# A two-layer decoder step: fewer plain head groups in the first attention stage, weight sums a stage later, the second chunk's norm in two passes through memory

## The chip, the cores and the metric

The kernel runs on one core of a Trainium2 chip. The time is device microseconds of one execution. A core has TensorE (matmuls, PE in the profile, its weight loads PEld), VectorE (DVE), ScalarE (ACT), GpSimd (POOL) and SyncE (SP). Each engine runs its own instructions in their order and waits on semaphores for the others. In this kernel SP starts the loads and the outputs, POOL starts nearly all stores to scratch memory.

## The reference

One step of a small decoder for 1024 prompt positions and 8 decode rows, model width 2048, in float32. Layer A: `z = x @ w_in`, half of z goes through causal pooling windows (2, 4, 8, 16) and a grouped projection, is gated by SiLU of the other half, and projected by `w_out`. Then `x = layer_norm(ALPHA * x + y)`. Its output gives one shared key and value (4 heads of 64). Layer B: queries and a gate from `z = h @ w_in_b`, sliding-window attention (128 keys) of 32 query heads with a learned sink, gate, projection and layer norm again:

```python
xp, sp = pool_layer(xp, prefix_p, pos_p, w_in_a[i], w_grp_a[i], scale_a[i], w_out_a[i], ln_g[i], ln_b[i])
k_p, v_p = shared_kv(xp, pos_p, w_kv)
xp = attn_layer(xp, pos_p, kb_p, vb_p, kpos_p, qpos_p, True, w_in_b[j], sinks_b[j], w_out_b[j], ln_g[i], ln_b[i])

def layer_norm(x, g, b):
    xf = x.astype(jnp.float32)
    mu = jnp.mean(xf, axis=-1, keepdims=True)
    var = jnp.mean(jnp.square(xf - mu), axis=-1, keepdims=True)
    return ((xf - mu) * lax.rsqrt(var + LN_EPS) * g.astype(jnp.float32) + b.astype(jnp.float32)).astype(x.dtype)
```

## The kernel before

**Chunks and phases.** Tokens lie along the free dimension, channels along the 128 partitions. The tokens are cut into chunk 0 (512) and chunk 1 (520: 512 and the 8 decode rows). `PHASES` (L50) lists ten phases in the order in which they run: input projection of layer A (`ai`), output projection of A (`ao`), input projection and attention of B (`bi`), output projection of B (`bo`). The third number of an `ai` or `bi` phase is the range of groups. A group of `bi` is four query heads and their gates: two pairs of weight rows, `wib` p (queries) and `wib` 8+p (gates), each pair four blocks of 128 x 1024.

**Exact matmuls in three.** Every weight block and every input tile is split into a rounded part (`hi`, a cast on ACT, L488 for weights) and the rest (`lo`, a subtraction on VectorE, L503 for weights). A block product is then three matmuls: hi by hi, hi by lo, lo by hi.

**Plain and seven products.** A plain unit (`unit`, L672 on) multiplies a block with all 512 tokens: 24 matmuls of 512 columns for each of a pair's four blocks (lines 686 to 688). A phase that is not in `PLAIN` uses a seven-product scheme for a 2 x 2 block product (`seven`, L582 on): seven weight blocks of 24 matmuls over half of the tokens, 256 or 260 columns (lines 658 to 660). Each has a post on ACT or VectorE that moves or combines the banks (L599 to L631). Three of the blocks are weights as they are, four are sums of blocks: `first_pair` (L332) makes the sums on VectorE from the loaded blocks (L346) and stores them in memory through POOL (L347). `plain_pair` (L300) makes and stores the same sums late (L293, L294) while the blocks are used plain. `next_pair` (L323) loads the sums in a later phase. The input of a seven-product phase needs four combinations too: `t_ops` (L820) makes them from a pair of tiles by four VectorE instructions (L826 to L829) and stores them through POOL (L830), `th` for the input of `bi`.

**Order.** `build_stream` lists all weight blocks in the order of use. At each block `begin` (L515) loads some blocks ahead (`load_to`), splits some ahead (`prep_to`: L503, `cast_to`: L488) and makes sums ahead. `end` (L527) runs events due at this block: the steps of the attention and, every `self.every` blocks, one step of the side generators, if enough slots are free. The side generator of this case is `ln_gen` (L912), the layer norm of a finished chunk. For chunk 1 it runs beside `bi` of chunk 0: mean, subtract (L962), square (L965), add (L968), variance, then for each of eight tile pairs multiply (L1000), affine on ACT (L991), store of the output through SP (L992) and `t_ops`. `in_order` ties PE, DVE and ACT to the source's order.

**Slots.** All working tiles come from 54 slots (`Mem`, L135) of 128 x 1040 floats. `full()` hands out the free slot that was let go longest ago; one that is being stored (`free(True)`) counts as let go ten turns later. The name of a tile in the order is `m`, the slot, the number of the allocation, and an id, so `m12_1836_16098` is slot 12. Who writes a slot anew waits for its last reader, a store included.

## Time and profile before

| | |
|---|---|
| median of 3 runs | 2332.18 us (2332.04 to 2333.17) |
| profiled execution | 2332.49 us, span 2330.7 us |
| TensorE busy, granted clock | 2293.2 us, 0.997 |
| VectorE busy | 1908.7 us |
| plain stage of `bi`, chunk 0 (4 groups) | 1080.6 to 1336.2 us |
| seven-product stage of `bi`, chunk 0 (4 groups) | 1336.2 to 1528 us |
| `bi`, chunk 1 | 1528 to 1961 us |

The busy time of TensorE is that of overlapping matmuls, so its pace is read from distances of starts, and its gaps from the idle time. The rows by stage give for each engine the busy time in a stretch. A group row gives the line, engine, tiles and shape, the count, the busy time and the mean of one, and behind the second bar the idle time before them and what ended it.

### The profile page before, as it was taken

The numbers are of one execution on the slowest core, as the hardware profiler recorded it, in microseconds if no ns is written. First come the engines' busy times: TensorE is split into PE (matmuls) and PEld (weight loads), VectorE is DVE, ScalarE is ACT, GpSimd is POOL, SyncE is SP. The second block draws the span as 40 slices with busy tenths as digits, with TensorE's granted clock in tenths as the row PEclk, the third lists the DMA queues.
The fourth block names the chain that finished last, engine by engine and source line by source line (L and its number), as shares of the span: only waits on it lengthen the run. The fifth ranks groups of instructions, "written<-read, shape, count | busy, mean of one in ns | idle before, by whom it ended". The sixth has DMA issues, their size and how long they took to land. (4 is left out here: it accounts for less than half of the span.)

```text
span 2330.7 us, 49775 instructions
## 1 busy us (share of the span) xinstructions
PE 2293.2 (98%) x19960; PEld 2199.7 (94%) x19960; DVE 1908.7 (82%) x2422; ACT 1350.4 (58%) x2492; POOL 205.7 (9%) x411
## 2 busy tenths in 40 slices
PE   8999999999999999999999999999999999999997
PEld 6899999999999999999788799999999999999997
DVE  8787998777878878988996888897676777889887
ACT  4444445544546546655465566785776678646556
POOL 0111110010000000000111111100000000000001
PEclk9999999999999999999999999999999999999999
DMA  8668789988899989999886666798777778799785
GB/s 293 221 228 312 267 293 356 330 302 297 278 325 320 340 280 325 323 385 345 274 333 240 241 220 236 240 321 288 246 245 221 221 229 307 243 361 379 250 303 198
DMA packets 250919, 665.04 MB, mean 285 GB/s; under 512 B 25760, under 2 KB 106432, under 8 KB 250688
## 3 DMA queue, kind: packets, MB, share of 16 engines
q1 hardware_dynamic: 205216, 496.79, 63.5%
q0 software_dynamic: 45472, 165.07, 18.4%
q8 instruction: 156, 2.56, 0.4%
q14 instruction: 75, 0.61, 0.1%
HBM read 466.66 MB, written 185.59 MB: 280 GB/s over the span
## 5 line engine op out<-in xcount | busy, mean ns | idle before, releaser
L658 PE MATMUL pD<-m,m 128*128 128x260 f32 (+1 forms) x4752 | 1346.2, 283 | 5.5 <-DVE m L619 3.9
L660 PE MATMUL pD<-m,m 128*128 128x260 f32 (+1 forms) x4752 | 1339.1, 282 | 3.3 <-DVE m L503 3.1
L659 PE MATMUL pD<-m,m 128*128 128x260 f32 (+1 forms) x4752 | 1339.3, 282 | 0.0
L658 PEld LDWEIGHTS pD<-m,m 128*128 128x128 f32 x4752 | 895.3, 188 | 10.9 <-issue 3.2
L660 PEld LDWEIGHTS pD<-m,m 128*128 128x128 f32 x4752 | 895.8, 189 | 4.0 <-DVE m L503 3.9
L659 PEld LDWEIGHTS pD<-m,m 128*128 128x128 f32 x4752 | 895.6, 188 | 0.5
L503 DVE TENSOR_TENSOR m<-m,m 128x1024 fp32r<-128x1024 f32 x674 | 814.6, 1220 | 72.7 <-ACT m L488 48.3
L488 ACT CAST m<-m 128x1024 fp32r<-128x1024 f32 x674 | 701.5, 1048 | 253.1 <-DVE m L346 77.7
L686 PE MATMUL pD<-m,m 128*128 128x512 f32 x448 | 179.7, 401 | 8.0 <-ACT m L769 8.0
L687 PE MATMUL pD<-m,m 128*128 128x512 f32 x448 | 177.6, 396 | 0.7 <-DVE m L778 0.7
L688 PE MATMUL pD<-m,m 128*128 128x512 f32 x448 | 177.2, 396 | 0.0
L778 DVE TENSOR_TENSOR m<-m,m 128x1024 fp32r<-128x1024 f32 (+1 forms) x120 | 147.1, 1229 | 9.5 <-ACT m L769 7.9
L631 ACT COPY m<-pD 128x260 f32<-128x260 f32 (+1 forms) x83 | 31.0, 374 | 189.8 <-PE pD L660 189.7
L769 ACT CAST m<-m 128x1024 fp32r<-128x1024 f32 (+1 forms) x120 | 125.8, 1051 | 10.3 <-DVE m L503 4.1
L346 DVE TENSOR_TENSOR m<-m,m 128x1024 f32<-128x1024 f32 x88 | 107.6, 1223 | 6.9 <-DMA m<-in_wia 4.2
L686 PEld LDWEIGHTS pD<-m,m 128*128 128x128 f32 x448 | 85.0, 190 | 27.9 <-ACT m L769 8.0
L687 PEld LDWEIGHTS pD<-m,m 128*128 128x128 f32 x448 | 85.0, 190 | 20.6 <-DVE m L778 1.9
L688 PEld LDWEIGHTS pD<-m,m 128*128 128x128 f32 x448 | 84.8, 189 | 19.8
L619 DVE TENSOR_TENSOR m<-pD,m 128x260 f32<-128x260 f32 (+1 forms) x86 | 36.5, 425 | 80.9 <-PE pD L660 80.8
L1798 ACT ACTIVATE m<-m,sm 128x128 f32<-128x128 f32 x256 | 99.2, 390 | 0.0
L1820 ACT ACTIVATE m<-m,sm 128x128 f32<-128x128 f32 (+1 forms) x320 | 93.9, 372 | 8.9 <-DVE sm L1806 5.5
L1088 PE MATMUL pD<-m,m 128*128 128x260 f32 (+1 forms) x528 | 91.2, 323 | 0.0
(249 smaller groups left out, 2157.2 us busy)
## 6 DMA issues: line engine op xcount, KB each, us to landing
m<-in_wia SPq DMA_DIRECT2D x124, 512.0 KB
m<-in_wib SPq DMA_DIRECT2D x120, 512.0 KB
swia<-m POOLq DMA_DIRECT2D x64, 512.0 KB, 5.0
m<-swia SPq DMA_DIRECT2D x64, 512.0 KB
m<-swoa SPq DMA_DIRECT2D x64, 512.0 KB
swib<-m POOLq DMA_DIRECT2D x64, 512.0 KB, 5.8
m<-swib SPq DMA_DIRECT2D x64, 512.0 KB
m<-swob SPq DMA_DIRECT2D x56, 512.0 KB
```

What stands on the lines that cost most here:

```text
L346: self.nc.vector.tensor_add(s[out].a[:, :1024], s[x].a[:, :1024], s[y].a[:, :1024])
L488: self.nc.scalar.copy(hi.r[:, :1024], self.stream[self.cast].src().a[:, :1024])
L503: self.nc.vector.tensor_sub(lo.r[:, :1024], s.src().a[:, :1024], hi.a[:, :1024])
L658: nc.tensor.matmul(ps[:, :TH], wh[:, s], h, start=new and k == 0, stop=False, skip_group_check=on)
L659: nc.tensor.matmul(ps[:, :TH], wh[:, s], l, start=False, stop=False, skip_group_check=on)
L660: nc.tensor.matmul(ps[:, :TH], wl[:, s], h, start=False, stop=k == 7, skip_group_check=on)
L686: nc.tensor.matmul(ps[:], wh[:, s], h, start=par == 0 and k == 0, stop=False)
L687: nc.tensor.matmul(ps[:], wh[:, s], l, start=False, stop=False)
L688: nc.tensor.matmul(ps[:], wl[:, s], h, start=False, stop=par == 1 and k == 7)
L769: self.nc.scalar.copy(h.r[:, :n], s.a[:, :n])
L778: self.nc.vector.tensor_sub(l.r[:, :n], s.a[:, :n], h.a[:, :n])
L1798: nc.scalar.activation(x["s3"][:, i, :], x["s3"][:, i, :], AF.Exp, bias=nm[:, i : i + 1], scale=0.125, accum_out=rs[:, i : i + 1],)
```

## The change

The first attention stage (`bi`, chunk 0) does groups 0 and 1 plain and groups 2 to 7 in seven products; before it was four and four. The plain groups no longer make their weights' sums. The stage of chunk 1 makes those of groups 0 and 1 itself, from the blocks, without storing them (`first_pair` with `keep=False`).

The norm of chunk 1 goes through memory: after the mean is subtracted and the square taken, tile pairs 0 to 6 are stored and let go. A second pass begins at count 56 after the phase's start (`self.i`, in which a plain block counts twice and a product of the seven once), that is 8 products into the seven-product stage. It loads the pairs again and for each pair does multiply, affine and `t_ops`, a step every 2.4 products.

`begin` now looks at free slots: it loads five blocks ahead and goes on to seven only while more than two slots are free, and splits one block less ahead with one slot free or none.

```diff
-    ("ai", 0, (0, 1)), ("ai", 0, (1, 4)), ("ai", 1, (0, 4)), ("ao", 0, None), ("ao", 1, None), ("bi", 0, (0, 4)),
-    ("bi", 0, (4, 8)), ("bi", 1, (0, 8)), ("bo", 0, None), ("bo", 1, None),
+    ("ai", 0, (0, 1)), ("ai", 0, (1, 4)), ("ai", 1, (0, 4)), ("ao", 0, None), ("ao", 1, None), ("bi", 0, (0, 2)),
+    ("bi", 0, (2, 8)), ("bi", 1, (0, 8)), ("bo", 0, None), ("bo", 1, None),
...
-    def first_pair(self, name, q):
+    def first_pair(self, name, q, keep=True):
...
-                self.nc.gpsimd.dma_start(ws[:, i, :], s[out].a[:, :1024])
+                if keep:
+                    self.nc.gpsimd.dma_start(ws[:, i, :], s[out].a[:, :1024])
...
-                if seven:
-                    for p in range(*part):
-                        w += pr("wib", p) + pr("wib", 8 + p)
-                else:
-                    for p in range(*part):
-                        q, g = pr("wib", p), pr("wib", 8 + p)
+                for p in range(*part):
+                    if not seven:
+                        q, g = ([self.lone(a) for a in self.quads("wib", n)] for n in (p, 8 + p))
                         w += q[:2] + g[:2] + q[2:] + g[2:]
+                        continue
+                    for n in (p, 8 + p):
+                        if c and p < PLAIN[1][2][1]:
+                            f = self.first_pair("wib", n, False)
+                            w += [f[i] for i in ORDER7]
+                        else:
+                            w += pr("wib", n)
...
         a, b, d = self.ahead if self.strassen else (5, 4, 3)
-        if getattr(self, "ph", "") == "bi1" and len(self.mem.whole()) < 3:
-            a, b, d = min(a, 6), min(b, 3), min(d, 2)
-        self.load_to(self.e + a)
-        self.prep_to(self.e + d)
-        self.cast_to(self.e + b)
-        self.make_to(self.e + b + (1 if self.strassen else 0))
+        free = lambda: len(self.mem.whole())
+        self.load_to(self.e + min(a, 5))
+        while self.loaded < min(self.e + a, len(self.stream)) and free() > 2:
+            self.load_to(self.loaded + 1)
+        self.prep_to(self.e + (d if free() > 1 else d - 1))
+        self.cast_to(self.e + (b if free() > 1 else b - 1))
+        self.make_to(self.e + (b if free() > 0 else b - 1) + (1 if self.strassen else 0))
...
                     nc.scalar.activation(flat(sqs[p - 1]), flat(pre[p - 1]), AF.Square)
+                    if p < 8:
+                        nc.gpsimd.dma_start(away(p - 1), self.pair_view(pre[p - 1], T))
+                        pre.pop(p - 1).free(True)
...
+        if c:
+            while self.i < self.mark:
+                yield
+            load(6)
...
+        if c:
+            turns = (6, 7, 0, 1, 2, 3, 4, 5)
+            for n, p in enumerate(turns):
+                if n < 7:
+                    load(turns[n + 1])
+                t = self.pair_view(pre[p], T)
+                nc.vector.tensor_mul(t, t, b2(rr))
+                yield
+                affine(p)
+                yield
+                self.t_ops(t[:, 0], t[:, 1], td, p, T // 2)
+                pre[p].free(True)
+                yield
...
             elif (kind, c) == ("bi", 0) and not self.strassen:
+                self.mark = self.i + 56
...
+            elif (kind, c) == ("bi", 0):
+                self.every, self.room = 2.4, 2
```

How VectorE's order changes is seen at two places. Lines 503, 826 to 829 and 1000 of before are lines 508, 832 to 835 and 1015 after the change. The first place is the second pass of the norm. Before, it stands in the plain stage, between plain blocks; `m51` holds the factor of the norm:

```order
L1000 TENSOR_TENSOR m24_1555_13007<-m24_1555_13007,m51_1536_12865 128x1040
L503 TENSOR_TENSOR m10_1627_13710<-m12_1617_13596,m16_1623_13665 128x1024
L826 TENSOR_TENSOR m44_1630_13736<-m29_1549_12967 128x260
L827 TENSOR_TENSOR m44_1630_13736<-m29_1549_12967 128x260
L828 TENSOR_TENSOR m44_1630_13736<-m29_1549_12967,m44_1630_13736 128x260
L829 TENSOR_TENSOR m44_1630_13736<-m29_1549_12967,m44_1630_13736 128x260
L1000 TENSOR_TENSOR m0_1562_13056<-m0_1562_13056,m51_1536_12865 128x1040
L503 TENSOR_TENSOR m41_1632_13764<-m3_1621_13661,m43_1628_13712 128x1024
```

Here the sums for `th` lie in slot 44, and the next split goes into slot 41. The second place is the fourth product of group 5, in the seven-product stage. Before:

```order
L1791 TENSOR_TENSOR sm_283_15815<-sm_282_15814,prm_75 128x8
L503 TENSOR_TENSOR m21_1810_15824<-m3_1787_15502,m35_1807_15786 128x1024
L503 TENSOR_TENSOR m39_1813_15862<-m22_1799_15655,m32_1811_15826 128x1024
L346 TENSOR_TENSOR m22_1799_15655<-m22_1799_15655,m3_1787_15502 128x1024
L1926 SCALAR_TENSOR_TENSOR m23_1798_15653<-m36_1808_15820,m23_1798_15653 128x1024
```

and after the change (L1818 is L1791 of before, L1953 is L1926):

```order
L1818 TENSOR_TENSOR sm_285_16057<-sm_284_16056,prm_75 128x8
L508 TENSOR_TENSOR m20_1834_16064<-m1_1812_15769,m36_1832_16028 128x1024
L832 TENSOR_TENSOR m12_1836_16098<-m29_1791_15501 128x260
L833 TENSOR_TENSOR m12_1836_16098<-m29_1791_15501 128x260
L834 TENSOR_TENSOR m12_1836_16098<-m29_1791_15501,m12_1836_16098 128x260
L835 TENSOR_TENSOR m12_1836_16098<-m29_1791_15501,m12_1836_16098 128x260
L508 TENSOR_TENSOR m12_1839_16110<-m32_1827_15985,m10_1835_16066 128x1024
L346 TENSOR_TENSOR m32_1827_15985<-m32_1827_15985,m1_1812_15769 128x1024
```

The four sums for `th` have moved in ahead of the split of this product, and the split writes slot 12, the one that they filled.

13 lines of the change are left out of this document (7 added, 6 removed).

## The prediction

> **What bounds the kernel now.** I read the page's busy shares first, then the table of stages, then what TensorE waits for in the two stages that the change touches.
>
> ```profile
> span 2330.7 us, 49775 instructions
> ...
> PE 2293.2 (98%) x19960; PEld 2199.7 (94%) x19960; DVE 1908.7 (82%) x2422; ACT 1350.4 (58%) x2492; POOL 205.7 (9%) x411
> ```
>
> TensorE (PE) is idle for 2330.7 - 2293.2 = 37.5 us of the span, so the whole kernel runs at TensorE's pace. The next table has one row for the plain attention stage of chunk 0, one for its seven-product stage, one for the attention stage of chunk 1.
>
> ```profile
> core 0: us, PE busy (x) PEld busy (x) DVE busy (x) ACT busy (x) POOL busy (x), PEclk, DMA share, GB/s
> ...
> 1080.60:1336.20 255.60, 252.89 (x1639) 205.56 (x1638) 211.77 (x281) 134.85 (x303) 38.62 (x79) 0.99 0.78 276
> 1336.20:1528.00 191.80, 189.58 (x2108) 185.48 (x2107) 169.51 (x204) 136.04 (x320) 24.45 (x55) 1.00 0.73 246
> 1528.00:1961.00 433.00, 432.00 (x4768) 424.66 (x4767) 322.83 (x447) 303.20 (x721) 25.49 (x54) 1.00 0.78 251
> ```
>
> In all three TensorE has gaps of 1 to 3 us, at a granted clock of 0.99 to 1.00. VectorE (DVE) is the engine behind it: 83%, 88% and 75% busy. So two questions decide: how much matmul time goes, and whether VectorE still feeds TensorE with two more groups at the dense pace.
>
> **The matmuls.** Around the border of the two stages the timeline of TensorE shows both paces, as distances of starts (the durations overlap).
>
> ```profile
> 1335.26 0.39 PE L688 MATMUL pD<-m,m 128*128 128x512 f32 x1
> ...
> 1336.19 0.28 PE L658 MATMUL pD<-m,m 128*128 128x256 f32 x1
> ...
> 1337.94 0.28 PE L658 MATMUL pD<-m,m 128*128 128x256 f32 x1
> ```
>
> Four plain matmuls of 512 columns take 1336.19 - 1335.26 = 0.93 us, 0.2325 each; the fifteen of 256 columns after them take 1.75 us, 0.1167 each. A group of heads has 8 weight blocks of 24 matmuls in plain form (192 x 0.2325 = 44.6 us) and 14 blocks in the seven-product form (336 x 0.1167 = 39.2 us). Two groups move: 384 matmuls leave (89.3 us), 672 come (78.4 us), **-10.9 us**. The attention matmuls themselves stay.
>
> **VectorE's load.** The groups of VectorE's work in the seven-product stage, and then two of the norm in the plain stage:
>
> ```profile
> L503 DVE TENSOR_TENSOR m<-m,m 128x1024 fp32r<-128x1024 f32 x56 | 67.5, 1218 | 4.4 <-PE pD L659 2.9 <-ACT m L488 0.8 <-PE pD L660 0.4
> L346 DVE TENSOR_TENSOR m<-m,m 128x1024 f32<-128x1024 f32 x29 | 35.4, 1222 | 1.7 <-DMA m<-in_wib 1.2
> ...
> L1000 DVE TENSOR_TENSOR m<-m,m 128x1040 f32<-128x1040 f32 x8 | 9.8, 1229 | 0.0
> L829 DVE TENSOR_TENSOR m<-m,m 128x260 f32<-128x260 f32 (+1 forms) x11 | 4.7, 428 | 0.4
> ```
>
> Two groups add 2 x 6 splits of 1.22 us (14.6) and 4 + 4 evictions of about 0.42 (3.4), and the 16 block sums of these groups (19.6 us) leave for the stage of chunk 1, which has 433 - 323 = 110 us to spare; without that cover they would cost up to 19.6. What matters is where the second pass of the norm now lies. Its 8 multiplies and 8 x 4 sums for the transformed input stood in the plain stage; the order has them in the second to fifth of the six dense groups, two pairs to a group. One pair is a multiply (1.23) and four sums, whose starts lie 0.34 apart in the timeline below. That is 2.6 us, so 5.2 per group. What a group of 14 products has now is seen in two stretches of 48 us, beside one of an earlier dense stage:
>
> ```profile
> 984.00:1032.00 48.00, 48.00 (x402) 48.00 (x401) 46.93 (x63) 28.27 (x40) 4.79 (x9) 1.00 1.00 390
> 1384.00:1432.00 48.00, 47.36 (x490) 46.41 (x489) 42.72 (x51) 32.91 (x85) 6.58 (x14) 1.00 0.73 255
> 1432.00:1480.00 48.00, 48.00 (x551) 47.44 (x551) 42.68 (x54) 34.10 (x84) 6.70 (x15) 1.00 0.72 236
> ```
>
> A group takes 191.8 / 4 = 47.95 us on TensorE and 42.7 on VectorE; with the norm it is 47.9. So VectorE is full, but the first row shows that full is enough: at 46.9 of 48 us TensorE had no gap. The load alone costs nothing; it takes away the 5.3 us per group in which VectorE could make up for a wait.
>
> **The waits that the change adds.** Slots run short: the norm's reloaded tiles and the seven-product inputs share the 54 slots, and by the kernel's own table of slots most products of the five groups begin with one slot free, where it was mostly two to seven. So a slot is written again as soon as it is let go. At three places the split of a weight block (L503, now L508) writes into the very slot from which the four sums just before it are still being stored: nothing lies between. At a fourth place one split lies between (1.2 us), at a fifth a split and a sum (2.4 us); there it is the sums' slot too. The store is issued by POOL and has to land first. How long that takes, by the transfers' rows: the norm's store in the plain stage, two kinds in the dense stage, and at last the spread over all stores of line 830:
>
> ```profile
> th<-m POOLq DMA_DIRECT2D x8, 520.0 KB, 5.8
> ...
> swib<-m POOLq DMA_DIRECT2D x29, 512.0 KB, 3.8
> ...
> to<-m POOLq DMA_DIRECT2D x4, 512.0 KB, 6.4
> ...
> DMA to landing us min/median/max: 2.9/7.0/9.3
> ```
>
> I take 5.8, the store's own; 6.4 is the same kind of store in the dense stage. VectorE then stands still for 3 x 5.8 + (5.8 - 1.2) + (5.8 - 2.4) = 25.4 us. Two casts on ACT (1.05 us each) write into such a slot too, with 5.0 us of VectorE's work between the store's last sum and the split that needs the cast: 2 x (5.8 + 1.05 - 5.0) = 3.7. Sum 29.1 us. Ends: 2.9 gives 3 x 2.9 + 1.7 + 0.5 = 10.9 us and nothing for the casts; 9.3 gives 27.9 + 8.1 + 6.9 + 10.7 = 53.6.
>
> [...]
>
> Behind a waiting split stand, in VectorE's order, the next sums and splits, the row maxima of the attention and the evictions (L619, L624), for which TensorE waits within a product. How much lead there is shows in the timeline of the dense stage:
>
> ```profile
> 1433.86 2.35 DVE L503 TENSOR_TENSOR m<-m,m 128x1024 fp32r<-128x1024 f32 x2
> ...
> 1436.81 0.28 PE L658 MATMUL pD<-m,m 128*128 128x256 f32 x1
> ...
> 1440.41 0.36 PE L658 MATMUL pD<-m,m 128*128 128x256 f32 x1
> ...
> 1446.35 0.43 DVE L619 TENSOR_TENSOR m<-pD,m 128x256 f32<-128x256 f32 x1 [1.30 <-PE pD L660]
> 1446.69 1.22 DVE L503 TENSOR_TENSOR m<-m,m 128x1024 fp32r<-128x1024 f32 x1
> 1447.82 2.48 DVE L346 TENSOR_TENSOR m<-m,m 128x1024 f32<-128x1024 f32 x2
> ...
> 1450.88 0.42 DVE L826 TENSOR_TENSOR m<-m 128x256 f32<-128x256 f32 x1
> 1451.21 0.42 DVE L827 TENSOR_TENSOR m<-m 128x256 f32<-128x256 f32 x1
> 1451.55 0.42 DVE L828 TENSOR_TENSOR m<-m,m 128x256 f32<-128x256 f32 x1
> ```
>
> Counted from the stage's start, the first split of the first row (31st of the stage, third of its group) belongs to the product whose first matmul is the second row: it ended at about 1435.1, 1.7 us ahead. The second split of that row ended at 1436.2 for the product of the third row, 4.2 us ahead. A stop of 5.8 us there reaches TensorE at once. Before, the lead came back in waits like the 1.30 us of L619, 5.3 us per group; now that room is filled. So TensorE loses the 29.1 us less the first lead (1.7), less four groups' rest of 0.05 (0.2), less the fifth stop (3.4), behind which the last group has no norm and VectorE catches up: **+23.8 us**. At 2.9 it is 10.9 - 1.7 - 0.2 - 0.5 = 8.5, at 9.3 it is 53.6 - 1.7 - 0.2 - 6.9 = 44.8.
>
> **At nothing.** ACT gets 12 casts, 20 evictions and the norm's affine in the dense stage; it is at 136 of 192 us there. The norm's 7 extra stores and 7 extra loads (520 KB each) stand against 16 stores and 4 loads of weight blocks less, at DMA shares of 0.73 and 0.78; without this cover a store on which nobody waits still costs nothing, and a late load would hold the norm, not the products. The new limits on loading ahead swap three loads in SP's order before the plain stage, and move nothing there on PE, DVE or ACT. In the last stage a few steps of the other norm swap places; I count nothing, and bound it by one such step, 1.2 us either way.
>
> **Sum.** 2332.49 (the profiled execution) - 10.9 + 23.8 = 2345.4; the median, 2332.18, lies 0.3 lower: 2345.1. Since the lead varies by place (1.7 and 4.2 us above), a part of one or two stops will be hidden, and I say **2344 us**. With landings of 3.8 to 6.4: at 3.8 VectorE stands for 11.4 + 2.6 + 1.4 = 15.4, TensorE loses 12.1; at 6.4 it stands for 19.2 + 5.2 + 4.0 + 4.9 = 33.3, TensorE loses 27.4. So 2333 to 2349 about the same mechanism.
>
> **Rivals.** (1) *The stops are hidden*: VectorE has more lead than at the place that I read, or is slowed less by the norm, and only the matmuls count: 2332.2 - 10.9 = 2321.3, faster. For it: the stretch at 98% without a gap, and the lead of 4.2 us. Against it: the 1.7 us, and that three stops have no work in between. It decides if a stop of 5 us opens no gap in TensorE. (2) *Stores land fast*: with fewer plain blocks around, a store lands in 2.9 to 3.8 us, as the weight sums in the dense stage do; the stops then give back what the matmuls saved: 2332.2 - 10.9 + 8.5 to 12.1 = 2330 to 2333, no change. [...] Against it: the four stores of 6.4 in that same stage. (3) *One free slot makes everything wait*: casts and splits also wait for the matmuls of the product just ended, and VectorE's waits of today (5.3 us per group) stay beside the new work in place of being filled by it; four groups, 21 us on top: 2365. For it: the depth of splitting ahead falls from three products to two wherever one slot is left. Against it: a VectorE that is late finds those matmuls done.
>
> **Chances.** The forecast 0.58 (its own range 2334 to 2356), (1) 0.17, (2) 0.15, (3) 0.10. Leaving out the lowest and the highest tenth gives 2322 to 2358. What a measurement can tell from no change is about 0.2%, 4.7 us: faster is (1) and the edge of (2), 0.19; the same is most of (2) and the low edge of the forecast, 0.16; slower is the rest, 0.65.
>
> **What would show it.** The plain stage ends about 2 x 53 us earlier after it began (255.6 less 2 x 8 blocks of 5.6 us and their attention), and six dense groups follow. Right: in the second to fifth of them VectorE has three waits of 4 to 6 us ahead of L508 that end with the landing of a "th" store, two of 3 to 5, and behind each TensorE has a gap of some us before L508's product or at a release by L625; VectorE is over 95% busy or waiting for DMA there. Wrong: these waits are under 2 us, or they stand without a gap in TensorE; then (2) or (1). If TensorE's gaps are spread over all products and end with ACT's casts, it is (3). If the seven-product pace in the moved groups is above 0.12 us, the first term was mis-sized.

## The result and the profile after

| | before | after |
|---|---|---|
| median | 2332.82 us | 2385.89 us |
| profiled execution | 2332.49 us | 2384.16 us |
| plain stage of `bi`, chunk 0 | 255.6 us (4 groups) | 153.5 us (2 groups) |
| dense stage of `bi`, chunk 0 | 191.8 us (4 groups) | 344.0 us (6 groups) |
| from `bi`, chunk 1, to the last seven-product matmul | 778.0 us | 783.3 us |

The changed kernel is slower: ratio 1.0227, 95% interval 1.0216 to 1.0238. (One execution at a granted clock of 0.66 took 3180.5 us; it is in the median of six, not in the ratio, and the median of the other five is 2384.16 us.) I had forecast 2344 us: the direction was right, the size was not, 53 us against 12.

The page's span and busy times of the changed kernel:

```profile
span 2382.4 us, 50347 instructions
...
PE 2306.1 (97%) x20248; PEld 2226.6 (93%) x20248; DVE 1925.0 (81%) x2434; ACT 1365.3 (57%) x2514; POOL 200.1 (8%) x402
```

TensorE is busy for 12.9 us more although 10.9 us of matmuls are gone: it multiplied more slowly in part of the time. The table of stretches, one row per dense group, shows where (columns as in the prediction; the figure before the last two is the granted clock):

```profile
core 0: us, PE busy (x) PEld busy (x) DVE busy (x) ACT busy (x) POOL busy (x), PEclk, DMA share, GB/s
1233.00:1283.50 50.50, 48.61 (x545) 47.07 (x545) 43.09 (x52) 31.98 (x66) 6.73 (x15) 1.00 0.67 235
1283.50:1341.50 58.00, 49.65 (x474) 47.63 (x473) 47.24 (x59) 35.48 (x86) 7.13 (x15) 0.94 0.71 255
1341.50:1407.30 65.80, 54.82 (x546) 53.28 (x545) 47.49 (x63) 36.18 (x87) 7.73 (x17) 0.90 0.64 217
1407.30:1471.30 64.00, 52.94 (x547) 51.40 (x546) 47.37 (x63) 36.02 (x87) 7.73 (x17) 0.92 0.63 216
1471.30:1528.60 57.30, 51.05 (x546) 49.02 (x545) 46.02 (x62) 34.92 (x86) 7.70 (x17) 0.94 0.69 239
1528.60:1577.00 48.40, 48.06 (x549) 47.30 (x548) 41.80 (x53) 37.85 (x89) 5.05 (x12) 1.00 0.81 266
```

The four groups with the norm's second pass take 57 to 66 us, the last group, without it, 48.4 (before: 47.95). In these four the clock is 0.90 to 0.94 on average, where before it was 1.00. What TensorE, VectorE and ScalarE (ACT) waited for in the dense stage (us in all, times, longest):

```profile
PE pD L664 <- ACT pD L605: 12.5, 5, 6.3
PE pD L666 <- DVE m L508: 10.4, 8, 2.9
PE pD L1890 <- ACT m L620: 9.7, 4, 3.5
PE pS L1788 <- DVE m L1756: 5.5, 2, 3.9
...
DVE m L508 <- DMA th<-m: 15.3, 4, 5.2
...
ACT m L493 <- DMA to<-m: 14.6, 2, 8.4
...
ACT m L620 <- DVE m L1756: 8.8, 3, 2.9
...
ACT m L493 <- DMA th<-m: 7.3, 2, 4.6
```

The splits (L508) wait for "th" stores as forecast. The casts (L493) wait as well, for "th" and for "to" (the same four sums of gated attention outputs, for the input of the output projection), and more of TensorE's waits end with ScalarE than with VectorE. The timeline shows the longest such stop, in the fourth group:

```profile
1434.94 0.53 POOL L836 DMA_DIRECT2D to<-m  x1 [0.81 <-DVE m L630]
...
1434.27 0.37 ACT L637 COPY m<-pD 128x256 f32<-128x256 f32 x1
1443.05 1.04 ACT L493 CAST m<-m 128x1024 fp32r<-128x1024 f32 x1 [8.41 <-DMA to<-m]
...
1445.66 0.36 ACT L605 ACTIVATE pD<-pD 128x256 f32<-128x256 f32 x1
...
1446.07 0.58 PE L664 MATMUL pD<-m,m 128*128 128x256 f32 x1 [6.26 <-ACT pD L605]
...
1446.66 0.42 PE L666 MATMUL pD<-m,m 128*128 128x256 f32 x1
...
1447.94 0.41 PE L666 MATMUL pD<-m,m 128*128 128x256 f32 x1
```

A cast writes into the slot from which the "to" sums are still leaving, and stands for 8.4 us. Behind it in ScalarE's order, after some operations of the attention, stands L605, the post that copies a bank and that TensorE needs at once. TensorE has a gap of 6.26 us, and its first matmul afterwards takes 0.58 us, twice the 0.28 of the prediction's rows. From 1446.66 to 1447.94 lie six matmuls, 0.213 us each, where the prediction's rows have 0.1167. The stretches around it:

```profile
1446.10:1452.90 6.80, 6.80 (x37) 6.80 (x38) 1.95 (x5) 4.10 (x12) 0.54 (x1) 0.59 0.79 280
1452.90:1458.50 5.60, 5.60 (x49) 5.26 (x48) 4.50 (x6) 3.44 (x8) 0.00 (x0) 1.00 0.21 85
```

The trace's record of the clock has it at half for 6.8 us, from inside the gap on; 5.6 us of that lie behind the gap (0.59 is the mean of the first stretch). At 0.213 in place of 0.1167 us per matmul, 45% of such time is lost. This gap is paid twice: by its length of 6.26 us, and by the 5.6 us of half clock behind it.

### The profile page after: what moved, and what is told of

It reads as the page before. It is cut to its first block, busy times and chain, and to the rows that moved or that the text cites. A ratio compares the mean times of both kernels' runs of the same rounds, so it can differ in the third digit from the quotient of the medians.

```text
span 2382.4 us, 50347 instructions
## 1 busy us (share of the span) xinstructions
PE 2306.1 (97%) x20248; PEld 2226.6 (93%) x20248; DVE 1925.0 (81%) x2434; ACT 1365.3 (57%) x2514; POOL 200.1 (8%) x402
## 3 DMA queue, kind: packets, MB, share of 16 engines
q0 software_dynamic: 44176, 160.41, 17.4%
## 5 line engine op out<-in xcount | busy, mean ns | idle before, releaser
L664 PE MATMUL pD<-m,m 128*128 128x260 f32 (+1 forms) x4976 | 1414.1, 284 | 19.9 <-ACT pD L605 13.5
L666 PE MATMUL pD<-m,m 128*128 128x260 f32 (+1 forms) x4976 | 1407.0, 283 | 14.9 <-DVE m L508 14.5
L665 PE MATMUL pD<-m,m 128*128 128x260 f32 (+1 forms) x4976 | 1406.0, 283 | 0.0
L508 DVE TENSOR_TENSOR m<-m,m 128x1024 fp32r<-128x1024 f32 x686 | 828.6, 1219 | 93.6 <-ACT m L493 53.4
L493 ACT CAST m<-m 128x1024 fp32r<-128x1024 f32 x686 | 714.2, 1048 | 302.9 <-DVE m L346 99.5
L346 DVE TENSOR_TENSOR m<-m,m 128x1024 f32<-128x1024 f32 x120 | 146.7, 1223 | 8.4 <-DMA m<-in_wia 4.7
L637 ACT COPY m<-pD 128x260 f32<-128x260 f32 (+1 forms) x87 | 32.5, 373 | 189.3 <-PE pD L666 189.2
L692 PE MATMUL pD<-m,m 128*128 128x512 f32 x320 | 128.9, 403 | 8.1 <-ACT m L775 8.1
L775 ACT CAST m<-m 128x1024 fp32r<-128x1024 f32 (+1 forms) x120 | 125.8, 1053 | 12.4 <-DMA m<-in_x 4.2
L693 PE MATMUL pD<-m,m 128*128 128x512 f32 x320 | 127.5, 398 | 0.5 <-DVE m L784 0.5
L694 PE MATMUL pD<-m,m 128*128 128x512 f32 x320 | 127.4, 398 | 0.0
L1115 PE MATMUL pD<-m,m 128*128 128x260 f32 (+1 forms) x528 | 91.3, 323 | 0.0
L614 ACT COPY m<-pD 128x260 f32<-128x260 f32 (+1 forms) x90 | 33.6, 373 | 82.5 <-PE pD L666 82.2
```

Source lines behind the costliest of these rows:

```text
L346: self.nc.vector.tensor_add(s[out].a[:, :1024], s[x].a[:, :1024], s[y].a[:, :1024])
L493: self.nc.scalar.copy(hi.r[:, :1024], self.stream[self.cast].src().a[:, :1024])
L508: self.nc.vector.tensor_sub(lo.r[:, :1024], s.src().a[:, :1024], hi.a[:, :1024])
L664: nc.tensor.matmul(ps[:, :TH], wh[:, s], h, start=new and k == 0, stop=False, skip_group_check=on)
L665: nc.tensor.matmul(ps[:, :TH], wh[:, s], l, start=False, stop=False, skip_group_check=on)
L666: nc.tensor.matmul(ps[:, :TH], wl[:, s], h, start=False, stop=k == 7, skip_group_check=on)
```

## The experiments

The theory after the traces, **A**: slots of which too few are free are written again while a store still reads them; that stops VectorE and ScalarE; TensorE pays the gaps and the half clock behind them. Rivals: **B**, VectorE simply has too much work in four groups; **C**, it is the two groups that moved; **D**, it is the order in which the norm's steps now stand. Lines are those of the changed kernel where nothing else is said.

### The stores read another slot

```diff
-        nc.gpsimd.dma_start(dst[:, kp], t)
+        nc.gpsimd.dma_start(dst[:, kp], t if self.still is None else self.still.v(4, TH))
...
```

> The changed kernel, with one thing else: in the dense part of the first attention stage the stores of the sums th and to read a slot that nobody writes there (the norm's factor, a table of values), not the slot with the sums. Stores, their sizes and targets stay, and so does the order of TensorE, VectorE and ScalarE; the stored data are not the sums, so what later stages compute from them is not the reference's. No split or cast has to wait for a landing store of sums any more. Theory A (slots written again under a store stop VectorE and ScalarE; ScalarE's order then holds the posts that TensorE needs; TensorE pays the gaps and, behind the longer ones, runs at half clock): of the 38 us of gaps and 16 us of half clock in the dense part most goes; the dense part takes 290 to 300 us in place of 344, the whole 2332 to 2345. Theory B (VectorE has simply too much work in four dense groups; its waits for stores fill room that it would lose anyway): the whole stays above 2370, with gaps that end with VectorE's splits or posts.

2345.96 us, ratio 1.0056 (1.0041 to 1.0071): 38.2 us less than the changed kernel's 2384.16, and just above A's range, as is the dense stage. Three of its dense groups, and TensorE's waits there:

```profile
1283.60:1335.00 51.40, 47.89 (x474) 46.48 (x473) 46.90 (x59) 35.35 (x86) 5.53 (x12) 0.97 0.76 256
1335.00:1388.00 53.00, 48.54 (x547) 47.41 (x546) 47.06 (x63) 36.30 (x87) 6.12 (x14) 1.00 0.67 229
1388.00:1441.70 53.70, 49.89 (x547) 48.97 (x546) 47.63 (x63) 35.79 (x87) 6.13 (x14) 0.97 0.71 238
...
PE pD L1890 <- ACT m L620: 7.6, 3, 2.6
PE pD L664 <- ACT pD L605: 4.6, 5, 1.5
PE pS L1788 <- DVE m L1756: 1.6, 1, 1.6
```

The orders of TensorE, VectorE and ScalarE are the same, VectorE is as busy as in the changed kernel (46.9 to 47.6 here), and the dense stage takes 305.1 us in place of 344.0. TensorE's waits there fall from 38.7 to 14.3 us, half clock behind gaps from 31.9 us to 6.8 (by the traces' records of the clock). So A holds for the 39 us of the dense stage, and B for these does not. One reservation: stores that no longer need their sums start earlier; all eight of "th" and five of the six of "to" went out in the plain stage, so their traffic left the dense stage too. Against traffic as the cause: the transfers there are as dense as in the changed kernel (229 to 256 GB/s against 216 to 255).

17.4 us above six groups of 47.95 stay. Of them, more below.

### Four plain groups: second pass late, second pass early

```diff
-    ("ai", 0, (0, 1)), ("ai", 0, (1, 4)), ("ai", 1, (0, 4)), ("ao", 0, None), ("ao", 1, None), ("bi", 0, (0, 2)),
-    ("bi", 0, (2, 8)), ("bi", 1, (0, 8)), ("bo", 0, None), ("bo", 1, None),
+    ("ai", 0, (0, 1)), ("ai", 0, (1, 4)), ("ai", 1, (0, 4)), ("ao", 0, None), ("ao", 1, None), ("bi", 0, (0, 4)),
+    ("bi", 0, (4, 8)), ("bi", 1, (0, 8)), ("bo", 0, None), ("bo", 1, None),
```

> The changed kernel with four plain groups, as before; the rest of the change stays, and the norm's second pass falls into the four dense groups there (it begins 4 plain blocks ahead of them). By the table of slots nine slots of it are written again at once or one product later. Theory A: these cost as in the changed kernel, some 4 to 5 us each with the half clock behind them; with the two groups' matmuls 10.9 us more than there: 2370 to 2395. Theory C (the two groups that moved cost the time, since a dense group needs more of VectorE than a plain one): the dense part is 4 groups of 48 us as before, the whole 2333 to 2345.

The second kernel has, besides:

```diff
-                self.mark = self.i + 56
+                self.mark = self.i + 0
```

> As the run before it, but the norm's second pass begins at once after the first, so that it lies in the plain groups. By the table of slots no slot of it is written again within three products. Theory A: nothing is left but the stores of the norm's first pass (5 to 7 us in the changed kernel's plain stage) and the later sums (5 us in the later stages): 2335 to 2348, and no wait of ScalarE or VectorE for a store of sums in the dense part over 2 us. If the two passes through memory or the new limits on loading ahead cost by themselves, it stays above 2360. Theory C gives the same as for the run before it, 2333 to 2345; only together do the two runs tell A from C.

Late: 2395.74 us, ratio 1.0270 (1.0253 to 1.0288). Early: 2340.28 us, 1.0035 (1.0024 to 1.0045). A stretch of 190 us from the dense stage's start and the longest waits of ScalarE in it, first late, then early:

```profile
1337.30:1526.50 189.20, 157.66 (x1561) 151.10 (x1560) 140.31 (x177) 105.70 (x242) 22.06 (x48) 0.91 0.64 220
...
ACT m L493 <- DMA th<-m: 32.9, 4, 10.1
```

```profile
1337.80:1528.00 190.20, 189.15 (x2109) 185.71 (x2108) 167.85 (x203) 134.19 (x317) 24.62 (x55) 1.00 0.71 246
...
ACT m L493 <- DVE m L346: 13.1, 7, 4.1
```

Same matmuls and same norm, 55.5 us apart; 190 us are some three dense groups of the one and all four of the other, at a clock of 0.91 and of 1.00. With no group moved the loss is as large as in the changed kernel, 12 us more even (2395.74 against 2384.16), about the matmul time that its two groups save. C falls: it is where the second pass lies.

### VectorE stopped by itself

In the kernel before; `pulse(n)` is n maxima of a table with itself, 1024 columns each.

```diff
-                self.every, self.room = 1, 0
+                self.every, self.room = 1, 0; [self.at(k, lambda n=n: self.pulse(n)) for k, n in ((10, 3), (24, 4), (38, 5), (52, 6), (66, 7), (80, 8), (94, 10))]
```

> The kernel before, with seven stops put into VectorE's order in the stage of chunk 1, at 10, 24, 38, 52, 66, 80 and 94 counts after its start: 3, 4, 5, 6, 7, 8 and 10 operations of 1024 columns on a table, which leave its values as they are. It measures by itself what a stop of VectorE costs TensorE. Theory A: each opens a gap of its length (1.2 us per operation) less VectorE's lead of 2 to 4 us, and behind a gap of about 2.5 us or more TensorE's clock is half for 3.4 us, behind one of about 3.5 us or more for 6.8 us: gaps of some 25 to 30 us in all, half clock behind four or five of them with a loss of 10 to 17 us, the whole 2365 to 2380. Rival: the half clock in the changed kernel comes from something else (what VectorE or the transfers do there), and gaps by themselves leave the clock at full speed: 2355 to 2365 and no half clock behind them.

2373.61 us (two executions), ratio 1.0173 (1.0149 to 1.0196), within the range of A. The seven stops are 43 operations of 1.22 us, 52.6 us of VectorE; the shortest, of 3.7 us, opened no gap. TensorE's gaps in their stretch are 29.6 us, and the clock goes to half at four of the stops, for 30.7 us in all, of which some 28 lie behind the first gap of each. Two stretches, the first with a gap of 2.9 us, the second with the end of one of 6.1:

```profile
1660.50:1667.00 6.50, 3.60 (x83) 3.36 (x76) 6.43 (x9) 3.53 (x8) 0.10 (x1) 1.00 0.15 30
1886.90:1897.40 10.50, 6.61 (x94) 5.72 (x95) 9.54 (x14) 4.25 (x8) 0.30 (x2) 0.51 0.21 57
```

Nothing else was changed here, no store and no slot, so the half clock comes with the gap. Not with every one: at the first gap of 2.9 us above the clock stayed at 1.00.

### What the 17 us are not, and what part of them is

Four kernels on top of the one with another source, where `self.still` is the other slot. Without the norm's 32 sums:

```diff
-        nc.vector.tensor_sub(t[:, 1, :], E[:, a], E[:, b])
+        if self.still is None or self.still is self.kv[3]: nc.vector.tensor_sub(t[:, 1, :], E[:, a], E[:, b])
...
```

> As the run in which the stores of sums read another slot (2346 us), and the 32 sums of the norm's second pass in VectorE's order left out (the four operations of 260 columns per pair; the stores stay, so th holds other values still). It takes 4 x 0.34 x 8 = 11 us off VectorE in four dense groups and nothing else. Theory B for the rest (with the stops gone, the dense part still takes 305 us in place of 6 x 47.95 = 288, because VectorE with 47 us of work in a group cannot make up its waits for the other engines): the dense part falls by about as much as VectorE gets, 8 to 13 us, to 292 to 297, the whole to 2333 to 2339. Theory D (the rest comes from the order in which posts and casts stand, whatever VectorE's load): 2343 to 2348.

2344.82 us, 1.0053 (1.0038 to 1.0068). B falls for the rest too: 11 us of VectorE moved 1 us. Without the affine:

```diff
-                nc.scalar.activation(t[:, j], t[:, j], AF.Identity, bias=b, scale=g)
+                nc.scalar.activation(t[:, j], t[:, j], AF.Identity, bias=b, scale=g) if not c else None
```

> The run in which the stores of sums read another slot, with the norm's affine on ScalarE in the second pass left out (16 operations of 520 columns; the outputs of the norm for chunk 1 are then not the reference's). Slots and all other orders stay. Theory D', the affine stands ahead of casts and posts in ScalarE's order and holds them: some 10 us less, 2333 to 2340. Otherwise 2343 to 2348.

2346.33 us, 1.0060 (1.0046 to 1.0075): nothing is won. With the full depth of splitting:

```diff
-        self.prep_to(self.e + (d if free() > 1 else d - 1))
-        self.cast_to(self.e + (b if free() > 1 else b - 1))
-        self.make_to(self.e + (b if free() > 0 else b - 1) + (1 if self.strassen else 0))
+        self.prep_to(self.e + d)
+        self.cast_to(self.e + b)
+        self.make_to(self.e + b + (1 if self.strassen else 0))
```

> The run in which the stores of sums read another slot, with the depth of splitting, casting and making sums ahead kept at 3, 4 and 4 blocks wherever slots run short (the changed kernel goes one lower with one slot free); the limit on loads stays. If the lower depth is what is left (rival 3 of the prediction): 5 to 15 us less, 2331 to 2341. If it is not, or what it wins is lost to slots taken earlier: 2343 to 2350.

2345.06 us, 1.0058 (1.0043 to 1.0073): nothing is won. Without all of the second pass's work, the 32 sums as above and:

```diff
                 t = self.pair_view(pre[p], T)
-                nc.vector.tensor_mul(t, t, b2(rr))
...
-                nc.scalar.activation(t[:, j], t[:, j], AF.Identity, bias=b, scale=g)
+                nc.scalar.activation(t[:, j], t[:, j], AF.Identity, bias=b, scale=g) if not c else None
```

> The run in which the stores of sums read another slot (2346 us), with all the work of the norm's second pass left out: the 8 multiplies and 32 sums on VectorE and the 16 affine operations on ScalarE. Loads, stores and every slot stay. If the 17 us are the norm's work among the other steps (each piece small, all of it together too much): the dense part falls from 305 to 288 to 293 us, the whole to 2329 to 2336. If they come from the slots (whoever writes one waits for its last reader, TensorE and ScalarE among them) or from the lower depth of splitting: 300 us or more, 2340 to 2346.

2342.18 us, 1.0047 (1.0032 to 1.0062). In the profiled executions the dense stage takes 300.8 us, 4.3 less (the executions of the two kernels overlap, 2340.80 to 2347.11 and 2345.07 to 2348.85); 13 us stay with no work of the norm's second pass in it, so most of the rest is not D either. A wait of ScalarE is there to the tenth as in the changed kernel and in the one with another source:

```profile
ACT m L620 <- DVE m L1755: 8.8, 3, 2.9
...
PE pD L1889 <- ACT m L620: 7.3, 3, 2.5
```

(Lines behind 1015 are one lower in this kernel: 1755 is 1756, the last addition of the rope, which rotates the queries by their position, and 1889 is 1890, a matmul of the attention.) The orders show what it is. First VectorE, then ScalarE, slot numbers kept, in the kernel with another source:

```
L1756 TENSOR_TENSOR m11_1745_14904<-m11_1745_14904,m34_1758_15077 128x1024
L1756 TENSOR_TENSOR m22_1797_15545<-m22_1797_15545,m45_1810_15756 128x1024
L1756 TENSOR_TENSOR m12_1850_16230<-m12_1850_16230,m35_1863_16441 128x1024
L620 COPY m34_1771_15208<-pD_262_15047 128x256
L620 COPY m45_1824_15893<-pD_278_15726 128x256
L620 COPY m35_1877_16578<-pD_294_16411 128x256
```

Three times the post L620 writes into slot 34, 45 or 35, which the rope has just let go; it waits until the addition has read it, and TensorE has a gap of 2.4 to 2.6 us behind it. No store is involved; by these orders it is once more a slot written again at once, though no run takes just these three away. That is 7.3 us of gaps and, behind one of the three here and two in the kernel with another source, half clock of 3.4 us. Of the 13.1 us (300.8 less 6 x 47.95) some 4 stay open.

### Stores of "to" alone

The kernel with another source, where "th" goes from its own slot again:

```diff
-                self.still = L; self.t_ops(t[:, 0], t[:, 1], td, p, T // 2); self.still = None
+                self.t_ops(t[:, 0], t[:, 1], td, p, T // 2)
```

> The changed kernel, where only the stores of the sums to (the gate's) in the dense part read another slot; those of th read the slot with the sums again. Output of the last projection is then not the reference's. What I counted in the prediction were waits for th alone. Theory A': casts on ScalarE that wait for to count as much (14.6 us of ScalarE's waits in the changed kernel end with them, and the posts behind them hold TensorE): 10 to 22 us less than the changed kernel, 2364 to 2376. Theory A'': a cast is wanted late, only the splits' waits for th count: 0 to 4 us less, 2382 to 2386.

2384.91 us, 1.0226 (1.0210 to 1.0241): nothing is won. ScalarE's 14.6 us for "to" are gone, and others have taken their place:

```profile
DVE m L508 <- DMA th<-m: 31.7, 5, 9.3
...
ACT m L493 <- DMA th<-m: 15.0, 2, 9.1
```

In the changed kernel these two were 15.3 and 7.3. Of the 15.3, one thing has to be said: there a fifth split waits too, for 4.65 us until 1480.41; the profile names post L614, but a "th" store issued at 1476.17 landed after 4.0 us, just before. With it the splits' waits are 20.0 us, and the growth to 31.7 has one source: three of the stores that these splits wait for landed later, after 9.8, 8.5 and 5.6 us in place of 5.5, 2.9 and 4.1. Why they did, no run shows. ScalarE's growth of 7.7 us has another: its two waits begin at 1380.3 and 1445.1, 1.0 us before the "th" store is issued. In the changed kernel a stop for "to" of 6.2 and of 8.4 us came shortly ahead of them, so that they began 1.7 and 4.1 us after the store's issue. So the stop ahead had hidden part of the wait behind it. In the first experiment the "th" stores were taken away besides, and 39 us of the dense stage went.

### Complete kernels that free slots

Three kernels change the depths of loading, casting and splitting ahead in the dense stage (7, 4, 3 in the changed kernel, loads 5 with few slots free), and set them back behind it.

```diff
-                self.every, self.room = 2.4, 2
+                self.every, self.room = 2.4, 2; self.ahead = 5, 3, 2
```

> The changed kernel, complete, with one line else: in the dense part of the first attention stage it loads, casts and splits 5, 3 and 2 blocks ahead, not 7, 4 and 3. That leaves more slots free: by the table of slots none is written again within two products after it was let go with a store. Theory A: the stops go without any work left out; VectorE's load stays: about as the run with another source, 2340 to 2352. Rival: with one block less of lead every short wait reaches TensorE, and what the stops cost comes back as many small gaps: 2360 to 2385.

```diff
+                self.every, self.room = 2.4, 2; self.ahead = 4, 3, 3
```

> The changed kernel, complete, with one line else: in the dense part of the first attention stage it loads 4, casts 3 and splits 3 blocks ahead, not 7 (5), 4 and 3. VectorE keeps its lead of three products, which the run with 5, 3 and 2 took away. By the table of slots in the dense part: allocations of a slot at the very count at which it was let go, 14 under a store and 31 others in the changed kernel, 0 and 1 here; one count later under a store, 16 in the changed kernel, 0 here. Theory A, widened (a slot written again at once makes splits, casts, posts and copies wait for whoever still reads it, a store, TensorE or ScalarE): besides the stops by stores also most of the 17 us go that the run with another source had still above 6 x 47.95 us: the dense part 288 to 298 us, the whole 2328 to 2339. Theory D (those 17 us come from where the norm's steps stand): 2343 to 2350, as with another source. Rival: loading 4 ahead is too late, splits and casts wait for loads: above 2350.

```diff
+                self.every, self.room = 2.4, 2; self.ahead = 5, 4, 3
```

> The changed kernel, complete, with one line else: in the dense part of the first attention stage it loads at most 5 blocks ahead, not up to 7; casts and splits stay 4 and 3 ahead. By the table of slots no split there is written into a slot of sums at once or one product later (five in the changed kernel), and three casts are. Theory A: most of what the stores' stops cost goes, with no work left out: 344 us in the dense part become 305 to 318, the whole 2345 to 2360. Rival (the depth of loading is needed as much as the others): splits and casts wait for loads instead, above 2370.

2377.41 us, 1.0196 (1.0179 to 1.0213); 2387.52 us, 1.0239 (1.0220 to 1.0257); 2379.50 us, 1.0202 (1.0188 to 1.0215). All three expectations of A failed, and those of the rivals held. The waits that came instead, one fence for each in this order:

```profile
PE pD L666 <- DVE m L508: 28.7, 10, 4.0
```

```profile
DVE m L508 <- ACT m L493: 42.5, 45, 2.9
...
ACT m L493 <- DVE m L346: 70.8, 30, 5.4
```

```profile
ACT m L493 <- DMA m<-in_wib: 24.1, 8, 8.7
...
ACT m L493 <- DMA th<-m: 14.3, 5, 9.9
```

With a lead of two products TensorE waits for the splits themselves. In this kernel and the next no split or cast waits for "th" or "to" any more, but for one of 1.5 us: the stops went, and the time did not. With casts no further ahead than splits, every split waits for its cast, and casts for block sums. With loads only five ahead, casts wait for the weights, and still for "th". To see the price of that last depth without any stop by sums, the same line in the kernel with another source:

> The run in which the stores of sums read another slot (2346 us), with the line of the run before it: loads at most 5 ahead. Allocations of a slot at the very count at which it was let go by a reader that is no store fall from 31 to 17 in the dense part, the depths of cast and split stay. Theory A, widened (what is left above 6 x 47.95 us are splits, copies and posts that wait for TensorE or ScalarE to have read the slot they write): half or more of the 17 us go, 2330 to 2338. Theory D (it is the order of the norm's steps among the others): 2343 to 2350.

2370.16 us, 1.0159 (1.0146 to 1.0172), 24 us slower than with loads up to seven ahead. So each depth carries time by itself, and slots cannot be freed there; these runs do not contradict A, but of the complete kernels only those with an early second pass bear it out.

### The plain stage

The kernel with another source, without the stores of the norm's first pass:

```diff
-                        nc.gpsimd.dma_start(away(p - 1), self.pair_view(pre[p - 1], T))
+                        pass
...
```

> As the run in which the stores of sums read another slot, and the seven stores of the norm's first pass left out (the second pass then loads what stood in that memory before). Theory A for the plain stage: these stores fill the transfer engines from 1095 to 1118 us, and the four copies of halves between partitions that the rope needs land 11.7 us after their issue in place of 7.3; without them the gap of 4.7 us at 1128 and the half clock behind it go: 5 to 8 us less, 2338 to 2341. Rival: the copies are late for another reason, the gap stays, 2344 to 2347.

2340.07 us, 1.0033 (1.0020 to 1.0046), 5.9 us less than with the stores of the first pass; the dense stage begins 6.7 us earlier. The stretch in which these stores go out and the wait of the rope (L1622, now L1649) for its copies between partitions, before the change, after it, and without the stores:

```profile
1095.00:1118.00 23.00, 23.00 (x101) 18.64 (x100) 17.16 (x18) 10.02 (x12) 1.76 (x3) 1.00 0.82 260
...
DVE m L1622 <- DMA m<-m: 0.7, 1, 0.7
```

```profile
1095.00:1118.00 23.00, 23.00 (x101) 18.67 (x100) 12.82 (x14) 9.07 (x11) 3.40 (x6) 1.00 1.03 399
...
PE pS L1710 <- ACT m L2084: 4.9, 1, 4.9
...
DVE m L1649 <- DMA m<-m: 8.9, 1, 8.9
```

```profile
1095.00:1118.00 23.00, 23.00 (x101) 18.67 (x100) 18.18 (x20) 9.75 (x12) 1.81 (x3) 1.00 0.96 311
...
DVE m L1649 <- DMA m<-m: 3.5, 1, 3.5
```

With the stores the transfer engines' share is 1.03, without them 0.96. The rope begins 12.4 us after the first of its copies was issued, where it was 8.0 before and is 7.0 without the stores, and in the changed kernel TensorE has a gap of 4.9 us at 1128.8 with half clock of 6.8 us, 4.0 of it behind the gap; both are gone without the stores. Spreading the stores, in the complete kernel with depths 4, 3 and 3:

```diff
-                        nc.gpsimd.dma_start(away(p - 1), self.pair_view(pre[p - 1], T))
-                        pre.pop(p - 1).free(True)
+                        def send(p=p, s=pre.pop(p - 1)):
+                            nc.gpsimd.dma_start(away(p - 1), self.pair_view(s, T)); s.free(True)
+                        self.at(2 * p, send)
```

> As the run before it, and the stores of the norm's first pass go out 2, 4, ... 14 counts later, so that they lie some 8 us apart instead of 3. Theory A for the plain stage: the transfer engines are no longer full when the copies of halves for the rope are issued, the gap of about 5 us at 1128 falls under 2.5 us and the half clock behind it goes: 4 to 7 us less than the run before it. Rival: the stores only meet another rope's copies or the loads of weight blocks: no difference over 2 us.

2385.16 us, 1.0216 (1.0202 to 1.0230). Beside the kernel with 4, 3 and 3 (2387.52 us) TensorE's gap falls from 5.2 to 1.5 us and the dense stage begins 5.3 us earlier, as expected, but it takes 6 us longer, and of the whole only 2.4 us are left, less than was expected; the executions of the two kernels overlap.

### The small parts, and a kernel from what was learned

The later sums alone, the limits alone (both on the kernel before), and a new kernel:

```diff
+                    if not seven:
+                        q, g = ([self.lone(a) for a in self.quads("wib", n)] for n in (p, 8 + p))
...
+                            f = self.first_pair("wib", n, False)
```

> The kernel before, with the sums of the plain groups' weights a stage later and nothing else: four plain groups without sums, 32 sums (39 us of VectorE) in the stage of chunk 1. The prediction costed this move at nothing, with 110 us of room in that stage. Right: 2330 to 2334. If the later stages' 5 us come from it (half as many sums there in the changed kernel): 2337 to 2344, in the stage of chunk 1.

```diff
+        self.load_to(self.e + min(a, 5))
+        while self.loaded < min(self.e + a, len(self.stream)) and free() > 2:
+            self.load_to(self.loaded + 1)
+        self.prep_to(self.e + (d if free() > 1 else d - 1))
...
```

> The kernel before with the new limits on loading, casting and splitting ahead, and nothing else. The prediction counted nothing and bounded it by 1.2 us in the last stage: 2331 to 2334. If the later stages' 5 us come from it (a gap of 2.5 us with half clock behind it at the start of the last projection of chunk 0): 2335 to 2340, with that gap 1.3 us or more longer than before.

2336.68 us, 1.0013 (1.0004 to 1.0022), and 2332.25 us, 0.9998 (0.9989 to 1.0007). The later sums cost a little, twice as many of them some 4 us (1 to 5 by the interval); the limits cost nothing. In the profiled execution of the first (2338.79 us, its slowest) the later stages, counted as in the table of results, take 789.1 us, 11 more than before, and the stages ahead of them end 5 us earlier.

The new kernel has three plain groups that make their sums as before, the second pass right behind the first, and the first pass's stores spread:

```diff
+    ("bi", 0, (0, 3)), ("bi", 0, (3, 8)),
...
+                        self.at(2 * p, send)
...
+                self.mark = self.i + 0
...
+                self.every = 1.0
```

> A complete kernel from what was learned: three plain groups, that keep making their weights' sums as before; the norm in two passes, the second right behind the first (a step each count), so that nearly all of it lies in the plain groups; the first pass's stores 2 to 14 counts later; limits on loading ahead as changed. By the table of slots nothing is written again under a store within one product in the dense part. Theory A: half of the 10.9 us of matmuls is won, 5.4, and nothing else lost: 2325 to 2330, faster than both. Rival: three plain groups hold the whole norm beside their sums, VectorE is at about 88% there, and its waits open gaps: 2333 to 2345.

2356.37 us, 1.0090 (1.0071 to 1.0109): slower than both expectations. Its six executions spread from 2345.26 to 2360.48 us, and the profiled one is the fastest, so its trace shows about half of the loss only. The dense stage is clean there (238.0 us for five groups); the plain one has two gaps:

```profile
PE pO L1887 <- ACT m L1857: 6.6, 1, 6.6
PE pD L690 <- DVE m L504: 5.5, 1, 5.5
...
DVE m L1646 <- DMA m<-m: 10.1, 1, 10.1
DVE m L346 <- DMA m<-in_wib: 5.3, 1, 5.3
```

The second of them, at 1126 us, comes behind the rope's copies again; ahead of the first, at 1284 us, VectorE waits for the load of a weight block, and a cast on ScalarE for the sum that VectorE makes of it. No kernel tried here beats the one before the change.

## Why the prediction was wrong, point by point

The account of the profiled executions, in us:

| term | forecast | measured | from |
|---|---|---|---|
| matmuls | -10.9 | -10.9 | the last dense group, with no norm, takes 48.4 us for 47.95 |
| stops by stores | +23.8 | +38.9 | dense stage 344.0, with another source 305.1 |
| rest of the dense stage | 0 | +17.4 | 305.1 less 6 x 47.95 |
| plain stage | 0 | +4.6 | 153.5 less 148.9, which is 255.6 without two groups of 44.6 + 8.75 (a dense group's 47.95 - 39.2) |
| later stages | 0, at most 1.2 | +5.4 | 783.31 less 777.95 |
| ahead of and behind these | 0 | -3.7 | starts of the stages, end of the span |
| sum | +12.9 | +51.7 | 2384.16 - 2332.49 |

**Matmuls: right.** The pace in a group without the norm is what it was.

**The stops: the mechanism was right, and the step that failed is "TensorE loses the 29.1 us less ...".** It took the gap for the whole loss. TensorE's waits that went with another source are 38.7 - 14.3 = 24.4 us, beside a forecast of 23.8; with them went 25.1 us at half clock, some 11 us of lost time (45%), for which the sum had no term. The two make some 36 of the 38.9.

That the forecast of the gaps came so close is luck: two errors cancel. The five splits that it counted waited 20.0 us, not 25.4, and behind the four of them that waited 4.6 to 5.2 us TensorE's gaps are 2.2 and 0.7, 2.9, 1.8 and 0.7 us, 8.4 in all. VectorE had a lead of 2 to 4 us at each, and the sum took off one (1.7). ScalarE made up for it: its casts waited 7.3 us for "th", forecast at 3.7, and 14.6 for "to", which I had not looked for, and the gaps that end with L605, which stands behind them, fell from 12.5 to 4.6 us with another source.

**The rest of the dense stage was put at nothing and measured 17.4 us.** It is the largest single error, and the next two points are what is known of it.

**"Full is enough": wrong by some 4 us.** VectorE's load was forecast at 47.9 us per group and measured at 47.2 to 47.5 in the second to fourth. With the stops gone, taking all of the second pass's work out gives 4.3 us back in the profiled executions. The earlier stage with 46.9 of 48 that I quoted as proof has no attention beside it.

**That products begin "with one slot free" was read too narrowly.** I looked for slots of sums under a store, and missed those written by posts right after VectorE had read them: 7.3 us of gaps at L620, by the trace and the orders. This is rival 3, with its mechanism in part (others than the splits wait for a slot's last reader) though not its price: VectorE's waits of old did not come on top of everything, and the lower depth of splitting cost nothing.

**"A store on which nobody waits still costs nothing": wrong by 5 to 6 us.** Nobody waits for the first pass's stores, but beside them the rope's copies were there 12.4 us after the first was issued, and 7.0 without them.

**The later sums and the limits.** The limits cost nothing, as said. The sums were costed at nothing with 110 us of room; twice as many cost some 4 us. How the 5.4 us of the later stages divide is not settled: half of that run's cost is 2 us, half of what its later stages took longer is 5.6, and the late and the early kernel with four plain groups, which have as many sums there as that run, take 2.1 and 7.9 us longer in these stages.

**Rivals.** Rival 1 (hidden) is out as a whole: waits of 5.2 us on VectorE and 8.4 on ScalarE opened gaps of 2.9 and 6.3, though VectorE's lead hid more than half of its stops. Rival 2 (stores land fast) is out by the eight "th" stores of the dense stage:

```profile
DMA to landing us min/median/max: 2.9/5.1/6.8
```

The smallest of them, 2.9 us, fits the rival's 2.9 to 3.8; the median of 5.1 does not.

## What to carry to other kernels

Price a stop of TensorE by its gap plus what the clock takes behind it: here single gaps of over 3.2 us (in the changed kernel 3.41 to 6.26 us) had 2.7 to 6.2 us at half clock behind them (there 3.3 to 6.1), which at 45% lost is an estimate of 1.2 to 2.8 us more than their length, and single gaps under 1.6 us had none. Whether it pays to split one long stop into short ones no run here tried. Before work is moved into a stretch with few free buffers, list for every engine which of its instructions will write a buffer whose last reader (a store, a copy, another engine) is still at it, and what stands behind that instruction in its order. Depths of loading ahead are no reserve from which buffers can be taken: one to three blocks less left 2377 to 2388 us of the changed kernel's 2384, though the stops by stores were gone in two of the three kernels.

## What the runs showed of the hardware

**The clock.** Over all traces of this case I took TensorE's gaps, without the wait ahead of the first matmul, that have no other of over 0.7 us within 12 us (from start to start), and looked whether the granted clock went to half in them or within 3.6 us behind:

| gap, us | gaps | followed by half clock |
|---|---|---|
| 0.8 to 1.6 | 83 | 0 |
| 1.6 to 2.0 | 18 | 6 |
| 2.0 to 2.8 | 32 | 27 |
| 2.8 to 3.2 | 11 | 9 |
| 3.2 and over | 39 | 39 |

In the traces of the kernel before and the changed kernel alone, the rows are 6 gaps and 0, 2 and 1, 2 and 2, 1 and 1, 5 and 5. The half clock lasts 3.4 us, or 6.8 at most gaps over 3.6, and can begin inside the gap. In the changed kernel it lasts 3.4 us at the single gaps of 2.47, 2.93 and 3.41 us and 6.8 us at those of 3.89, 4.12, 4.90 and 6.26 us; at the one of 6.26 us, from 1439.81 to 1446.07, it begins at 1444.8. Among the shorter gaps length alone does not decide: one of 1.82 us before the change (at 1324.8) was followed by it, one of 1.84 us in the changed kernel (at 1420.8) was not, nor was the gap of 2.9 us with VectorE stopped by itself.

**The transfers.** Beside the first pass's stores, at 399 GB/s, four copies of 128 KB between partitions were there 12.4 us after the first was issued, where they took 8.0 us at 260 GB/s before the change and 7.0 us at 311 GB/s with the stores left out. So the rate alone does not set it; that the stores do is what leaving them out shows. The first pass's stores of 520 KB took 5.8 to 9.7 us.
